# Stick-breaking attention with the keys on the partitions: suffix sums by triangle matmuls

## The chip, the cores and the metric

The kernel runs on one core of a Trainium2 chip. The metric is device time in microseconds of one execution, the median of three runs. A profile shows one execution: its span runs from the first to the last instruction, and its own time is a little longer than the span.

## The reference, cut to what matters

The kernel is one decoder block on a sequence of 1024 tokens with 1024 channels, in float32: a conditioned norm, one wide input projection, a state-space branch and an attention branch beside each other, a gated merge, an output projection, and a feed-forward part. The change concerns the attention branch alone: 8 heads of 64 channels, strictly causal, with stick-breaking weights instead of a softmax:

```python
z = einsum('bhqd,bhkd->bhqk', qb, kh) * scale
mask = key_pos < q_pos
log_not = where(mask, log_sigmoid(-z), 0.0)
suffix = cumsum(log_not, axis=3, reverse=True) - log_not
weights = where(mask, exp(log_sigmoid(z) + suffix), 0.0)
out = einsum('bhqk,bhkd->bhqd', weights, vh)
```

For each query, the log of "stick not broken" is summed over all later keys. With s = softplus(z) = max(z, 0) + ln(1 + exp(-|z|)), log_sigmoid(-z) is -s and log_sigmoid(z) is z - s, so the weight of a key is exp(z minus the sum of s over that key and all later ones).

## The kernel before, in words

The block is built in Python and compiled with a framework that tracks tiles, inserts the waits, and orders each engine's instructions by a plan on simulated times. Program order gives priority; work that comes later in the program fills gaps as soon as its inputs, buffers and manual order allow. A manual order (the helper `after`) holds in the plan only and puts no wait into the program.

Precise matrix products are made from a rounded high part and a remaining low part of each operand (type fp32r, one pass) as three products: high x high, high x low, low x high. Scores and weights times values use plain fp32 matmuls, of which each appears as two instructions.

The attention stage handles the heads in four pairs (`hp`), two heads of a pair side by side (index `x`) in the upper and lower 64 rows or columns. For each pair, `heads` goes over four blocks `I` of 256 queries (the last pair in the order 1, 3, 2, 0), and `scores` (line 679) makes the weights of one block, with **queries on the partitions and keys along the free axis**. A block's scores are cut into units of 384 or 512 columns for both heads, 40 units in all. For each unit:

- line 699 and 703: score matmuls into the tile `z` in PSUM (one buffer of two banks), and a matmul of an identity with a mask on the diagonal;
- line 708: ScalarE copies `z` to `wa`; lines 709 and 710: VectorE makes |z| (`we`) and max(z, 0) (`wr`); lines 711 and 712: ScalarE makes ln(1 + exp(-|z|)) in `we`;
- line 715: VectorE scans both with adds along the keys, from the last key back, which gives the inclusive suffix sum in `wr`; a unit starts from the column where the one before ended (line 719 saves it);
- line 722: GpSimd subtracts it from the scores; line 723: ScalarE takes the exponential.

The product with the values needs the keys on the partitions. So `heads` transposes the weights in 128x128 pieces on TensorE (line 745, into three PSUM buffers `wtp`), copies them out (line 749, on ScalarE, every fourth on VectorE), and multiplies by `V` (line 755) into `av`. Line 758 splits the result into high and low parts.

Between this lies other work for TensorE, which the plan uses to fill gaps: the query and key projections of the next pair (`qk_proj`, pinned after a score matmul of the pair before by `QPIN`), which go through the one PSUM bank `mm`, and the eight gate projections (`gate`, lines 649 to 660, pinned along the stage by `PINS`), which go through the bank `mg_`. Both run on line 622. After the stage, `branch_b` projects the attention's output (line 886). It uses the banks `mm`, `mg_`, the three of `wtp` and the one of `av`.

## Time and profile before

| | us |
|---|---|
| three runs, median (lowest, highest) | 1612.36 (1609.24, 1612.84) |
| the profiled execution, its own time | 1616.59 |
| its span | 1614.7 |
| mean granted TensorE clock of the profiled execution | 0.952 |
| attention stage, from the first score matmul to the last weights times values | 415.2 to 770.5 |
| TensorE busy, of the span | 1462.5 |

In the views that follow, PE is TensorE's matmuls and PEld its weight loads, DVE is VectorE, ACT ScalarE, POOL GpSimd, SP SyncE. The granted clock is a share of TensorE's full speed. A group is all instructions of one line, engine, operation and tile name, and the line of a helper (622, for instance) can serve many callers. In a group's row, the busy time and the mean time of one instruction come first, and after the second bar the time in which the engine stood idle just before them and what ended it. In a list of waits, each row gives who waited for whom, the total, the number of times and the longest. Matmuls are pipelined: the time of one in a row is longer than the distance from one to the next.

### The profile page before, as it was taken

To read this page: it belongs to the slowest core of one execution; us is meant where nothing else is said; L and a number is where in the kernel's file an instruction comes from. 1 tells how busy PE (TensorE), PEld (TensorE's weight loads), DVE (VectorE), ACT (ScalarE), POOL (GpSimd) and SP (SyncE) were. 2 spreads that over 40 slices of the span, in tenths; PEclk is the share of its full clock that TensorE was granted. 3 is DMA by queue.
4 is the path that set the end of the run, shared out by engine and by line. 5 is a ranking of instruction groups with operands and counts; after the bars stand their busy time and mean duration, and the time that the engine had idled before them with its cause. 6 is when DMAs were issued, how large, how long until landed. Compare 5 with 4: busy or idle time off the path is not lost.

```text
span 1614.7 us, 18727 instructions
## 1 busy us (share of the span) xinstructions
PE 1462.5 (91%) x6802; PEld 1149.4 (71%) x6802; DVE 1149.4 (71%) x1402; ACT 616.2 (38%) x859; POOL 790.4 (49%) x591
## 2 busy tenths in 40 slices
PE   4897888899999999889999979999999998999965
PEld 3687776778756666556878758888888886887854
DVE  6988777543576667585742887666566759999978
ACT  4521110352455555465423543332322324343313
POOL 3457784010334243333430454545555468788784
PEclk9998998999999989999999979999999999999988
DMA  8585556634201121201643323333333146455302
GB/s 235 170 197 166 157 161 171 180 120 156 92 7 52 34 78 46 72 24 60 230 176 97 112 67 110 98 100 114 116 119 112 63 158 247 147 159 163 98 27 105
DMA packets 191141, 193.58 MB, mean 120 GB/s; under 512 B 28068, under 2 KB 141832, under 8 KB 191048
## 3 DMA queue, kind: packets, MB, share of 16 engines
q1 hardware_dynamic: 179976, 184.38, 37.1%
q10 hardware_dynamic: 11072, 8.00, 1.7%
q8 instruction: 54, 0.88, 0.2%
q14 instruction: 39, 0.32, 0.1%
HBM read 142.40 MB, written 48.76 MB: 118 GB/s over the span
## 4 chain that ended last, share of the span: by engine, by line
PE 27%; DVE 14%; issue 7%; POOL 5%; DMA 2%; ACT 2%; SPq 0%; DVEq 0%; POOLq 0%; ACTq 0%
PE tq L1041 10%; PE wo L1041 8%; PE wo L922 4%; PE gu L1041 3%; DVE wr L715 1%; POOL wb L1114 1%; DVE x L1129 1%; DVE f L1116 1%; POOL pb L1133 1%; POOL pa L1094 1%; DMA gb<-gD 1%; DVE pb L1129 1%; DVE wl L1112 1%; PE mm L622 1%; DVE we L709 1%
## 5 line engine op out<-in xcount | busy, mean ns | idle before, releaser
L722 POOL TENSOR_TENSOR wa<-wa,wr 128x1024 f32<-128x1024 f32 (+1 forms) x40 | 90.4, 2259 | 183.6 <-DVE wr L715 151.3
L433 POOL TENSOR_TENSOR ws<-wb 128x1024 f32<-128x1024 f32 x29 | 73.2, 2525 | 103.5 <-DVE wl L436 58.6
L715 DVE TENSOR_TENSOR_SCAN wr<-we,wr 128x512 f32<-128x512 f32 (+3 forms) x80 | 79.5, 1042 | 37.6 <-ACT we L712 37.0
L433 POOL TENSOR_TENSOR wgs<-wb 128x1024 f32<-128x1024 f32 x15 | 37.9, 2524 | 101.2 <-DVE x L436 33.4
L709 DVE TENSOR_SCALAR we<-wa 128x1024 int32<-128x1024 int32 (+1 forms) x40 | 53.5, 1338 | 28.4 <-ACT wa L708 28.4
L622 PE MATMUL mm<-pb,wh 128*128 128x512 f32 x192 | 63.2, 407 | 4.1 <-DVE gst L657 4.1
L622 PE MATMUL mm<-pa,wgh 128*128 128x512 f32 x176 | 61.6, 428 | 5.5 <-DVE gst L657 5.5
L1094 POOL TENSOR_TENSOR pa<-pa,row 128x1024 f32<-128x1024 f32 x22 | 64.9, 2975 | 1.5 <-DMA pa<-in_w_ffn_down_dram 1.5
L622 PE MATMUL mm<-pa,wh 128*128 128x512 f32 x192 | 64.1, 413 | 0.1
L1032 POOL TENSOR_TENSOR f<-f,f 128x512 f32<-128x512 f32 x30 | 49.1, 1662 | 26.0 <-DVE f L1022 17.5
L622 PE MATMUL mm<-pb,wgh 128*128 128x512 f32 x176 | 59.0, 413 | 2.6 <-ACT gst L659 2.6
L774 DVE SCALAR_TENSOR_TENSOR acc<-aw,cond,acc 128x512 f32<-128x512 f32 x56 | 52.4, 935 | 12.4 <-DMA aw<-in_w_ada_dram 11.8
L723 ACT ACTIVATE wa<-wa 128x1024 f32<-128x1024 f32 (+1 forms) x40 | 38.8, 971 | 57.4 <-POOL wa L722 57.4
L710 DVE TENSOR_SCALAR wr<-wa 128x1024 f32<-128x1024 f32 (+1 forms) x40 | 60.3, 1507 | 0.0
L755 PE MATMUL av<-wt,V 128*64 128x256 f32 (+1 forms) x320 | 55.5, 384 | 5.1 <-ACT wt L749 1.8
L745 PE MATMUL wtp<-ident,wa 128*128 128x128 f32 x288 | 49.5, 300 | 10.5 <-ACT wa L723 10.5
L711 ACT ACTIVATE we<-we 128x1024 f32<-128x1024 f32 (+1 forms) x40 | 38.9, 972 | 52.1 <-DVE we L709 52.1
L745 PEld LDWEIGHTS wtp<-ident,wa 128*128 128x128 f32 x288 | 34.5, 150 | 32.6 <-ACT wa L723 13.0
L417 POOL TENSOR_TENSOR wl<-ws,wh 128x1024 fp32r<-128x1024 f32 x10 | 25.1, 2516 | 64.4 <-ACT wh L414 64.4
L414 ACT CAST wh<-ws 128x1024 fp32r<-128x1024 f32 x30 | 31.3, 1048 | 65.5 <-PE wo L922 25.7
L699 PE MATMUL z<-k,q 64*128 64x512 f32 (+3 forms) x192 | 46.4, 545 | 4.3 <-ACT wa L708 2.4
L1114 POOL TENSOR_TENSOR wb<-pa 128x512 f32<-128x512 f32 x23 | 40.7, 1777 | 15.6 <-DVE wxl L1112 5.5
(739 smaller groups left out, 4781.4 us busy)
## 6 DMA issues: line engine op xcount, KB each, us to landing
aw<-in_w_ada_dram SPq DMA_DIRECT2D x32, 512.0 KB, 4.6
hD<-f SPq DMA_DIRECT2D x30, 512.0 KB, 3.1
wb<-in_w_ffn_gate_dram SPq DMA_DIRECT2D x44, 256.0 KB, 3.8
wb<-in_w_ffn_up_dram SPq DMA_DIRECT2D x44, 256.0 KB, 4.2
pa<-in_w_ffn_down_dram SPq DMA_DIRECT2D x22, 512.0 KB, 5.8
wb<-hD SPq DMA_DIRECT2D x40, 256.0 KB, 2.8
ws<-in_w_in_dram SPq DMA_DIRECT2D x19, 512.0 KB, 5.9
x<-in_x_dram SPq DMA_DIRECT2D x16, 512.0 KB, 7.1
```

The costliest lines, as they stand in the source:

```text
L433: (add or nc.gpsimd).tensor_tensor(st, a, b, op)
L622: self.nc.tensor.matmul(ps, lhsT=w[a][:, k], rhs=act[h][k][:, b], start=(j == 0), stop=(j == n - 1))
L709: nc.vector.tensor_scalar(s.bitcast(I32), a.bitcast(I32), 0x7FFFFFFF, None, ALU.bitwise_and)
L710: nc.vector.tensor_scalar(r, a, 0.0, None, ALU.max)
L715: nc.vector.tensor_tensor_scan(r[:, x, b:e][:, ::-1], s[:, x, b:e][:, ::-1], r[:, x, b:e][:, ::-1], nxt[x][j], ALU.add, ALU.add)
L722: nc.gpsimd.tensor_tensor(a, a, r, ALU.subtract)
L745: nc.tensor.transpose(ps[:, d, j], w[j][kb // 4][:, x, c:c + P], self.ident)
L755: nc.tensor.matmul(av[h, P * j.start:256], lhsT=V[:, kb + d, h], rhs=ts[x][:, d, j].rearrange("p j q -> p (j q)"), start=(kb + d == 0), st ...
L922: nc.tensor.matmul(ps, lhsT=mg[t // 4][k][:, a, P * (t % 4):P * (t % 4) + P], rhs=ws[k // 2][b][:, k % 2], start=(j == 0), stop=(j == 23))
L1041: self.nc.tensor.matmul(ps, lhsT=w[x][:, q, k], rhs=self.B[i](y, k), start=(j == 0), stop=(j == 11))
L1094: nc.gpsimd.tensor_tensor(w, w, g2, ALU.mult)
L1114: nc.gpsimd.tensor_tensor(st[:, R], u, W[p][b[0]][:, 512 * b[1]:512 * b[1] + 512], SIGN_B[i])
```

## The change

Scores are now made with **keys on the partitions and queries along the free axis**: the operands of the score matmul change places. `heads` goes over two blocks `Q` of 512 queries, and within each over the blocks of 128 keys from the last to the first; the two narrowest blocks at the diagonal share a unit. The softplus s is made as one tile (absolute value on ScalarE straight from PSUM, a copy of z on VectorE, exponential and logarithm on ScalarE, max and add on VectorE), and is rounded into a high and a low part.

The sum over later keys then runs along the partitions and is a matmul. A tile `acc` in PSUM (one bank for each head) holds a running sum. For each key block, a matmul with a triangle of ones (`upto`) adds the block's inclusive suffix sums; VectorE subtracts `acc` from the scores; and a matmul with the complement (`rest`) adds what is missing, so that every row holds the full sum of the block before the next one starts. The exponential of the result has the keys on the partitions already, so it goes straight into the product with `V`.

The scans, the GpSimd subtraction, the transposes and their copies are gone. Score tiles have two buffers in PSUM (four banks), `acc` has two banks, `av` takes the bank `mg_`, and the gates now go through `mm`, the same bank as the query and key projections. `branch_b` gets six banks of its own beside `mm` and `mg_`. The pins are set anew for 40 marks (one for each unit) in place of 64, and the last pair's order of blocks is as in the other pairs.

```diff
-ZPB, WTB, AVB = 1, 3, 1
-WEB, WRB, GB = 2, 2, 2
-WAB2, WTS = 5, 3
+ZPB = 2
+GB = 2
+WAB2, WSB, WHB = 4, 2, 2
-QPIN = -16
-PINS = (0, 8, 16, 24, 32, 40, 48, 56)
-HD = (0, 4)
-HORD = {3: (1, 3, 2, 0)}
+QPIN = -10
+PINS = (0, 5, 10, 15, 20, 25, 30, 35)
...
+    def triangles(self, pool):
+        tri = pool.tile([P, P], F32, name="tri")
+        nc.gpsimd.memset(tri, 1.0)
+        nc.gpsimd.affine_select(out=tri, in_=tri, compare_op=ALU.is_gt, fill=0.0, base=1, pattern=[[-1, P]], channel_multiplier=1)
+        self.upto, self.rest = (pool.tile([P, P], F32R, name=n) for n in ("upto", "rest"))
+        nc.vector.tensor_copy(self.upto, tri)
+        nc.vector.tensor_scalar(self.rest, tri, -1.0, 1.0, ALU.mult, ALU.add)
...
+    def scores(self, q, k, Q, kbs, work):
...
+                ins = nc.tensor.matmul(z[:, x, f:f + w], lhsT=k[h, P * kb:P * kb + P], rhs=q[h, 512 * Q + c:512 * Q + 512],
+                                       start=f == 0, stop=not diag)
...
+        nc.scalar.activation(st, z, AF.Abs)
+        nc.vector.tensor_copy(at, z)
+        nc.scalar.activation(st, st, AF.Exp, scale=-1.0)
+        nc.scalar.activation(st, st, AF.Ln, bias=1.0)
+        nc.vector.scalar_tensor_tensor(st, at, 0.0, st, ALU.max, ALU.add)
+        nc.scalar.copy(ht, st)
+        nc.vector.tensor_tensor(lt, st, ht.bitcast(F32), ALU.subtract)
+        return a, (hi, lo), segs
...
+        for Q in range(2):
+            kbs = [(4 * Q + 3, 4 * Q + 2), (4 * Q + 1,), (4 * Q,)] + [(kb,) for kb in reversed(range(4 * Q))]
+            acc = self.accp.tile([P, 2, 512], F32, name="acc")
+            av = self.avp.tile([P, 512], F32, name="mm")
+            for unit in kbs:
+                a, parts, segs = self.scores(q, k, Q, unit, work)
+                for kb, f, c in segs:
+                    first, last = kb == 4 * Q + 3, kb == 0
                     for x in range(2):
+                        for n in range(2):
+                            nc.tensor.matmul(acc[:, x, c], lhsT=self.upto, rhs=parts[n][:, x, f], start=first and n == 0, stop=last and n == 1,
+                                             skip_group_check=True)
+                        nc.vector.tensor_tensor(a[:, x, f], a[:, x, f], acc[:, x, c], ALU.subtract)
+                        if not last:
+                            for n in range(2):
+                                nc.tensor.matmul(acc[:, x, c], lhsT=self.rest, rhs=parts[n][:, x, f], start=False, stop=False,
+                                                 skip_group_check=True)
+                    self.last_exp = nc.scalar.activation(a[:, :, f], a[:, :, f], AF.Exp)
                     for x in range(2):
                         h = slice(64 * x, 64 * x + 64)
+                        nc.tensor.matmul(av[h, c], lhsT=V[:, kb, h], rhs=a[:, x, f], start=first, stop=last, skip_group_check=True)
+            s = slice(512 * Q, 512 * Q + 512)
             self.split(hi[:, s], lo[:, s], av)
...
-                            self.gate(1, m, gp, self.marks[PINS[m]] if m else None, self.wring[2], mg_)
+                            self.gate(1, m, gp, self.marks[PINS[m]] if m else None, self.wring[2])
...
-                    banks = Turns((mm, "mm"), (mg_, "mm"), *[(self.wtp, "wtp")] * WTB, *[(self.avp, "av")] * AVB)
+                    bb = s3.enter_context(self.pool("bb", 6, PSUM))
+                    banks = Turns((mm, "mm"), (mg_, "mm"), *[(bb, "bb")] * 6)
```

More of the change, by code (lines that the diff above doesn't have):

```diff
@@ L753, in heads @@
                     for x in range(2):
                         h = slice(64 * x, 64 * x + 64)
-                        nc.tensor.matmul(av[h, P * j.start:256], lhsT=V[:, kb + d, h], rhs=ts[x][:, d, j].rearrange("p j q -> p (j q)"),
-                                         start=(kb + d == 0), stop=(last and d == 1))
-            s = slice(256 * I, 256 * I + 256)
+                        nc.tensor.matmul(av[h, c], lhsT=V[:, kb, h], rhs=a[:, x, f], start=first, stop=last, skip_group_check=True)
@@ L1239, in run @@
                     op = s3.enter_context(self.pool("o", 4))
-                    self.zp, self.wtp, self.avp = (s3.enter_context(self.pool(n, b, PSUM)) for n, b in (("zp", ZPB), ("wtp", WTB), ("avp", AVB)))
-                    with self.pool("work", 1) as work, self.pool("wt", WTS) as wt:
+                    with self.pool("tri", 1) as tri, self.pool("work", 1) as work, self.pool("zp", ZPB, PSUM) as self.zp, self.pool("acc", 1, PSUM) as self.accp:
+                        self.avp = mg_
+                        self.triangles(tri)
                         self.marks = []
@@ L1252, in run @@
                             ops.append((t[:, 0], t[:, 1]))
-                            self.heads(hp, q, k, V, work, wt, *ops[hp])
+                            self.heads(hp, q, k, V, work, *ops[hp])
                         spare = []
```

95 lines of the change are left out of this document (25 added, 70 removed).

## The prediction, made blind

> **What bounds the kernel now.** I read the page's busy line first, then the busy time by stretch inside the attention stage, then the list of waits there, then the groups of that stage by line. The attention stage runs from the first score matmul at 415 us to about 766 us, where the projection of line 886 has begun. The change rewrites this stage and touches little else.
>
> ```profile
> PE 1462.5 (91%) x6802; PEld 1149.4 (71%) x6802; DVE 1149.4 (71%) x1402; ACT 616.2 (38%) x859; POOL 790.4 (49%) x591
> ```
>
> TensorE is the fullest engine of the kernel, but that is an average. The stage itself, as busy time by stretch (wall, then busy time and count of PE, PEld, DVE, ACT, POOL, then the granted clock):
>
> ```profile
> 480.00:498.70 18.70, 14.93 (x73) 9.11 (x71) 13.05 (x13) 12.34 (x17) 5.45 (x4) 1.00 0.37 98
> 498.70:505.60 6.90, 5.93 (x19) 5.06 (x20) 6.90 (x6) 3.94 (x6) 6.24 (x3) 0.51 0.10 38
> 505.60:560.00 54.40, 53.48 (x278) 34.73 (x276) 35.92 (x43) 31.99 (x49) 17.32 (x8) 1.00 0.09 25
> 560.00:570.40 10.40, 7.72 (x40) 4.91 (x38) 5.61 (x7) 5.80 (x8) 3.72 (x3) 1.00 0.01 2
> 570.40:580.60 10.20, 9.92 (x30) 6.34 (x31) 10.09 (x9) 6.02 (x7) 6.94 (x3) 0.50 0.65 180
> 580.60:640.00 59.40, 59.40 (x296) 39.95 (x296) 38.72 (x42) 31.98 (x49) 22.91 (x11) 1.00 0.17 54
> 415.00:766.00 351.00, 323.48 (x1551) 212.41 (x1552) 238.89 (x245) 198.07 (x284) 132.85 (x61) 0.94 0.15 45
> ```
>
> The last row is the whole stage: 351.0 us, PE busy 323.5, so 27.5 us idle. The mean clock of 0.94 means another 0.06 x 351 = 21 us in which PE worked at half rate and should not have had to. I call the sum, 48.5 us, the slack of the stage. The other rows show how the two hang together: PE idles 3.8 us in 480 to 498.7, and the next 6.9 us are granted half the clock; it idles 2.7 us in 560 to 570.4, and the next 10.2 us are at 0.50. The long stretches in between are full (59.40 of 59.40) at clock 1.00. Half clock here follows idling. In both half-clock stretches DVE is the full engine (6.90 of 6.90, 10.09 of 10.20). So the stage is bound by PE's work for most of its length, and in short pieces by the scan path behind it:
>
> ```profile
> POOL wa L722 <- DVE wr L715: 151.3, 33, 8.2
> ACT wa L723 <- POOL wa L722: 57.4, 24, 5.4
> PEld wtp L745 <- ACT wa L723: 13.0, 7, 5.7
> PE wtp L745 <- ACT wa L723: 10.5, 5, 4.9
> ```
>
> That is the chain: the scan (715) releases the subtraction on POOL (722), that the exponential (723), that the transposes (745). PE's largest wait, 10.5 us in five pieces, stands at its end.
>
> **The change part by part: PE.** The score matmuls keep their number and their widths with queries and keys exchanged: per pair of heads 24 of them, 12 of 512 columns and 4 each of 384, 256 and 128, as before; the 64 mask matmuls stay too. They cost nothing new. The rest needs these groups and prices (groups of the stage; then pieces of the chain with start, length and count; then one line of the timeline):
>
> ```profile
> L755 PE MATMUL av<-wt,V 128*64 128x256 f32 (+1 forms) x312 | 54.6, 385 | 5.1 <-ACT wt L749 1.8 <-DVE wt L749 1.6 <-DVE o L809 1.5
> L745 PE MATMUL wtp<-ident,wa 128*128 128x128 f32 x288 | 49.5, 300 | 10.5 <-ACT wa L723 10.5
> ```
>
> ```profile
> 683.97 1.01 PE av L755 x8
> ...
> 685.57 0.58 PE av L755 x2
> 686.15 1.02 PE wtp L745 x8
> ...
> 965.76 8.16 PE wo L1041 x36
> ```
>
> Removed: 288 transposes. Packed, one takes 1.02/8 = 0.1275 us, so 288 x 0.1275 = 36.7 us of work; what else stands in the group's 49.5 us is waiting and half clock, which I count as slack.
>
> Added: the suffix sums. Each key block of each head takes two matmuls with the triangle (high and low part), and all but the last block of a sweep two more with its complement. Per pair of heads that is 48 + 40 = 88, in all 352: 160 of 512 columns and 64 each of 384, 256 and 128. They are full-array fp32r matmuls like those of line 1041, where one of 512 columns takes 8.16/36 = 0.227 us. By columns the 384 wide one is 0.170; for 256 and 128 I take the 0.1275 of a packed 128 wide transpose as the floor. 160 x 0.227 + 64 x 0.170 + 128 x 0.1275 = 36.3 + 10.9 + 16.3 = 63.5 us.
>
> By the Trainium skill, "TensorE: Matmul & The Clock Gate", section "Back-to-back issue gap", a sustained stream needs about 131 ns per matmul at 512 columns and 81 ns at 128. An estimate from that page alone would make the added work about 37 us and the removed 23, a net of 14 where my rows give 27. The trace disagrees with its 131 ns: 36 matmuls in a row need 227 ns each, and I stay with the rows.
>
> Weights times values: the same columns in 96 matmuls of up to 512 instead of 160 of up to 256. An fp32 matmul is two instructions, and the two heads sit in different column halves of the array. Eight instructions for two key blocks of both heads take 1.01 us, so one block of both is 0.505; two instructions for one head alone take 0.58. The halves run side by side when both heads are ready together and cost double when not. Before, the heads' transposed copies come from separate evacuations, and the group is busy 54.6 us, where 64 x 0.505 + 16 x 0.25 = 36.3 would do if all were paired. After, both heads' weights come out of one exponential, so they always go as a pair. The gain lies between 0 and 18; I take 10, because some of the excess is half clock and must not be counted twice.
>
> PE's work: +63.5 - 36.7 - 10 = **+17 us** (+9 to +27 by the bounds of the last term).
>
> **The change part by part: DVE, ACT, POOL.** Their groups in the stage:
>
> ```profile
> L722 POOL TENSOR_TENSOR wa<-wa,wr 128x1024 f32<-128x1024 f32 (+1 forms) x40 | 90.4, 2259 | 183.6 <-DVE wr L715 151.3 <-DVE cy L719 13.4 <-ACT wa L708 9.4
> L715 DVE TENSOR_TENSOR_SCAN wr<-we,wr 128x512 f32<-128x512 f32 (+3 forms) x80 | 79.5, 1042 | 37.6 <-ACT we L712 37.0
> L710 DVE TENSOR_SCALAR wr<-wa 128x1024 f32<-128x1024 f32 (+1 forms) x40 | 60.3, 1507 | 0.0
> L709 DVE TENSOR_SCALAR we<-wa 128x1024 int32<-128x1024 int32 (+1 forms) x40 | 53.5, 1338 | 28.4 <-ACT wa L708 28.4
> L715 DVE TENSOR_TENSOR_SCAN wr<-we,cy,wr 128x512 f32<-128x512 f32 x16 | 19.6, 1269 | 7.8 <-ACT we L712 7.7
> L749 DVE COPY wt<-wtp 128x512 f32<-128x512 f32 (+2 forms) x29 | 13.0, 474 | 26.6 <-PE wtp L745 14.5 <-PE av L755 12.1
> L711 ACT ACTIVATE we<-we 128x1024 f32<-128x1024 f32 (+1 forms) x40 | 38.9, 972 | 52.1 <-DVE we L709 52.1
> L712 ACT ACTIVATE we<-we 128x1024 f32<-128x1024 f32 (+1 forms) x40 | 38.9, 972 | 0.6
> L723 ACT ACTIVATE wa<-wa 128x1024 f32<-128x1024 f32 (+1 forms) x40 | 38.8, 971 | 57.4 <-POOL wa L722 57.4
> L708 ACT COPY wa<-z 128x1024 f32<-128x1024 f32 (+1 forms) x40 | 37.1, 927 | 16.1 <-PE wtp L745 7.9 <-PE z L703 5.5 <-PE z L699 2.6
> L749 ACT COPY wt<-wtp 128x512 f32<-128x512 f32 (+2 forms) x83 | 32.6, 442 | 20.4 <-PE wtp L745 14.9 <-PE av L755 5.4
> L414 ACT CAST wh<-ws 128x1024 fp32r<-128x1024 f32 x8 | 8.3, 1046 | 0.0
> L657 DVE COPY gst<-mm 128x512 f32<-128x512 f32 x8 | 5.4, 680 | 8.6 <-PE mm L622 8.6
> ```
>
> ```profile
> 953.86 1.13 DVE wl L436
> ```
>
> ```profile
> 414.50 0.69 DVE L855 TENSOR_TENSOR gst<-ga,sg 128x512 f32<-128x512 f32 x1 [3.17 <-DMA nD<-gst]
> ```
>
> The number of units (score tiles) stays 40, of the same sizes: 24 with 1024 elements, 16 with 768. DVE loses 79.5 + 60.3 + 53.5 + 19.6 + 13.0 = 225.9 us. It gains per full unit a copy out of PSUM (twice the 0.68 of line 657 at most, say 1.3), a max-and-add and a subtraction of 1024 elements (1.13 each, the row of line 436) and two subtractions out of PSUM (0.69 each, line 855): 4.9 us; a smaller unit three quarters of that. 24 x 4.9 + 16 x 3.7 = 177 us, so DVE sheds about 49 and comes to 190 of 351. Its share cannot bind on average.
>
> ACT sheds the 32.6 of line 749 and gains the rounding copy, 24 x 1.05 + 16 x 0.79 = 37.7: +5, to about 203 us. The absolute value takes the place of the copy of line 708 at its price. POOL sheds 90.4 us, and its 2.3 us step falls out of each unit's chain. All three lie beside PE, which has over 320 us of work; they count only through the slack. The two triangles are four small instructions made once, and needed only after the first unit's six operations on ACT and DVE, about 1 us each by the rows above.
>
> New waits: PE's complement matmuls wait until DVE has read the running sum, and stand in PE's queue ahead of whatever follows, fillers (gate and query/key projections) included; DVE's subtraction can itself stand behind one 1.13 us operation. Both heads have a bank of their own, so the other head and the fillers can go in between. The projections of gates and queries/keys now share one bank: 28 evacuations, each beside attention work, so I cost them at nothing; without that cover it would be 28 x 0.7 = 20 us.
>
> **The sum.** The question is what is left of the 48.5 us of slack. The stalls sat where DVE was full and at the end of the scan-POOL-exponential chain; DVE gets 49 us lighter, POOL leaves the chain, two score tiles instead of one may be open. The new sum brings waits of its own. I take half, 24 us left, as the middle between none (a full PE, as in the stretches at 59.40 of 59.40) and all. Stage: 351 + 17 - 24.5 = 343.5, **-7.5 us**. Against the profiled execution's 1616.6 that is 1609; the median of the three runs lies 4.2 below the profiled one, so I predict **1605 us**.
>
> **The rivals.** (a) *The new sum stalls PE as the scan did*: slower. Its place is the 80 pairs of complement matmuls, which PE meets in order behind DVE's 0.69 us read and what DVE does before. If they wait 0.3 us each on average, 80 x 0.3 = 24 us come back, the slack stays at 48.5, and +17 of work is paid in full: 1612.4 + 17 = 1629; with unpaired heads, +27, 1639. It decides from a mean wait of about 0.1 us (8 us) upwards. For it: 27.5 us of idle now arise from just such handovers. Against: PE has projections of line 622 to put between (the same view, that line alone): 672 x 0.227 = 152 us of them.
>
> ```profile
> 415.00:766.00 351.00, 180.15 (x672) 127.96 (x672) 0.94 0.15 45
> ```
>
> (b) *All slack goes*: PE full, 5 us left: 351 + 17 - 43.5 = -26, 1586. For it: the full stretches; against: start and tail of the stage, where fillers are short. (c) *The clock alone*: if the transposes, not the idling, kept the clock down, taking them out would bring back 21 us with the idle time unchanged: +17 - 21 = -4, 1608. The Trainium skill, "TensorE: Matmul & The Clock Gate", Part 4, says that transposes don't count as busy for the clock. The trace speaks against it: 50 transposes (line 745 alone, below) lie in a stretch granted 1.00 throughout, and both shown drops follow idling.
>
> ```profile
> 580.60:640.00 59.40, 7.88 (x50) 5.51 (x50) 1.00 0.17 54
> ```
>
>  (d) *Nothing to measure*: work gained and slack lost cancel, 1612 within 3. That the edit doesn't do what it says can be left out: the instructions it names are gone or there.
>
> **How the numbers follow.** Forecast 0.34 (1592 to 1609), (b) 0.13, (c) 0.04, (d) 0.15, (a) 0.34. 0.2% is 3.2 us, about what a measurement here can tell. Faster: 0.34 + 0.13 + 0.04 less a little of the near end, 0.49; same 0.15; slower 0.36. Both signs hold much of the chance: the likeliest case's own range is 1592 to 1609. The range of all: down into (b), 1588; up into (a) past its 1629, 1634. The lower part of (b), and (a) with unpaired heads, stay out, about 2 in 10.
>
> **What would show it.** In the profile after: line 745's group gone, the triangle matmuls near 60 us at full clock; weights times values down from 54.6 towards 40; DVE in the stage near 190, POOL near 45; PE's idle time in the stage near 14 and its clock near 0.97. It is wrong if PE waits on DVE's subtraction for more than 20 us in all, if the stage stays at a clock of 0.94, if DVE's operations take well over 1.13 us, or if the tail after the last scores leaves PE idle for over 15 us.

## The result, and the profile after

| | before | changed |
|---|---|---|
| median of 11 runs each, side by side, us | 1609.71 | 1618.39 |
| lowest, highest | 1604.66, 1613.67 | 1613.42, 1624.63 |
| ratio (95% interval) | 1 | 1.0053 (1.0035 to 1.0071) |
| profiled execution: own time, span | 1616.59, 1614.7 | 1618.39, 1616.7 |

The change makes the kernel slower by 8.7 us, 0.5%, and the interval of the ratio lies clear of 1. The forecast was 1605 us, faster.

The two profiled executions differ by 1.8 us only, and that misleads. Up to the first score matmul the matmuls of both kernels stand in the same order, yet that part, which waits on transfers, lasted 415.3 us in the profile of before and 404.6 in that of the changed kernel; over all profiles of this study it lies between 402.4 and 415.5. So I compare from the first score matmul on. From there to the first matmul of the output projection (tile `wo`) the kernel before takes 399.2 us and the changed one 414.5, which is 15.3 more. From `wo` to the end of the span they take 800.2 and 797.6. The difference of the two is 12.7 us, a little more than the 8.7 of the medians; a second profile of the changed kernel, below, gave 415.9 from the first score matmul to `wo` and a ratio of 1.0078. Each such time comes from one profiled execution.

The page's busy line after:

```profile
PE 1475.8 (91%) x6738; PEld 1153.8 (71%) x6738; DVE 1106.9 (68%) x1399; ACT 626.6 (39%) x816; POOL 705.3 (44%) x553
```

PE gained 13 us of busy time over the page of before, DVE lost 43 and POOL 85: what was to become lighter did. Busy time by stretch of the stage, first score to last weights times values, in the changed kernel (columns as in the prediction):

```profile
404.60:440.00 35.40, 34.92 (x147) 24.07 (x148) 15.53 (x16) 17.95 (x22) 6.92 (x3) 0.81 0.18 52
440.00:480.00 40.00, 32.95 (x143) 18.54 (x144) 28.12 (x35) 29.50 (x34) 5.03 (x2) 0.96 0.00 1
480.00:520.00 40.00, 39.14 (x183) 25.85 (x181) 20.73 (x27) 20.64 (x25) 0.00 (x0) 1.00 0.15 40
520.00:560.00 40.00, 32.46 (x132) 16.72 (x131) 29.19 (x35) 32.51 (x37) 5.47 (x2) 0.91 0.08 27
560.00:580.00 20.00, 20.00 (x91) 13.60 (x90) 10.65 (x13) 11.57 (x13) 0.00 (x0) 1.00 0.08 27
580.00:740.00 160.00, 158.09 (x716) 108.67 (x715) 79.16 (x99) 78.30 (x93) 24.41 (x14) 1.00 0.19 61
740.00:769.50 29.50, 25.66 (x103) 14.48 (x101) 17.57 (x21) 18.49 (x19) 1.28 (x1) 1.00 0.07 27
404.60:769.50 364.90, 343.22 (x1506) 221.93 (x1506) 200.96 (x241) 208.96 (x242) 43.11 (x22) 0.97 0.14 43
```

The same from first score to last weights times values in the kernel before, a little longer than the stretch in the prediction:

```profile
415.20:770.50 355.30, 327.98 (x1575) 215.69 (x1575) 238.69 (x244) 199.33 (x286) 132.65 (x61) 0.94 0.16 48
```

By the prediction's way of counting, the slack before is 355.3 - 328.0 = 27.3 us of idle and 0.06 x 355.3 = 21.3 of half clock, 48.6 together; after, 364.9 - 343.2 = 21.7 and 0.03 x 364.9 = 10.9, 32.6 together. It fell by 16 us. What is left of the wall is PE's work: 306.7 before, 332.3 after, 25.6 more. The stage is 9.6 us longer for it. (The clock is printed with two digits, so a half-clock term, and with it the work, is good to about 2 us.) Some 7 us of the 10.9 lie at the head of the stage, where the first 14 us were granted 0.52 while PE was full (404.60 to 418.60, 13.99 of 14.00 busy), behind 1.8 us of idling ahead of the first score matmul; that part stands ahead of any wait for the new sum.

Two stretches hold most of the idle time, 440 to 480 and 520 to 560. PE works 32.95 and 32.46 of 40 us there, and no other engine is full either: DVE stands at 28 and 29, ACT at 30 and 33. Where nobody is full, the engines may be waiting for one another. The list of waits in the stage names whom:

```profile
DVE wa L738 <- PE acc L736: 87.0, 49, 6.0
ACT wa L743 <- DVE wa L738: 67.6, 27, 8.7
PEld acc L741 <- DVE wa L738: 27.9, 31, 2.2
PE acc L741 <- DVE wa L738: 12.2, 16, 1.8
```

Line 736 is the triangle, 738 the subtraction, 741 the complement, 743 the exponential. DVE waits for the triangles, PE for the subtraction, and both for each other within one key block, first for one head and then for the other. PE's 12.2 us are the largest part of its 21.7 us of idle time. (PE's and PEld's waits overlap and are not to be added.) Groups of the stage:

```profile
L738 DVE TENSOR_TENSOR wa<-wa,acc 128x512 f32<-128x512 f32 (+3 forms) x96 | 52.9, 552 | 87.5 <-PE acc L736 87.0
L717 DVE SCALAR_TENSOR_TENSOR ws<-wa,ws 128x1024 f32<-128x1024 f32 (+1 forms) x40 | 48.2, 1208 | 16.9 <-ACT ws L716 16.7
L719 DVE TENSOR_TENSOR wl<-ws,wh 128x1024 fp32r<-128x1024 f32 (+1 forms) x40 | 46.0, 1150 | 13.0 <-ACT wh L718 12.3
L746 PE MATMUL mm<-wa,V 128*64 128x512 f32 (+3 forms) x192 | 42.7, 524 | 1.3 <-ACT wa L743 1.2
L736 PE MATMUL acc<-wh,upto 128*128 128x512 f32 (+3 forms) x96 | 34.6, 360 | 1.6 <-DVE wa L738 1.6
L741 PE MATMUL acc<-wh,rest 128*128 128x512 f32 (+3 forms) x80 | 31.3, 392 | 12.5 <-DVE wa L738 12.2
```

Weights times values went from 54.6 us to 42.7. I call the way from the triangle on PE to the subtraction on DVE and back to the complement on PE a trip. It is in the timeline, PE and DVE at one narrow block at the diagonal:

```profile
525.99 1.22 DVE L714 COPY wa<-z 128x1024 f32<-128x1024 f32 x1
526.22 0.30 PE L736 MATMUL acc<-wh,upto 128*128 128x128 f32 x1 [1.41 <-DVE wa L738]
526.36 0.28 PE L736 MATMUL acc<-wl,upto 128*128 128x128 f32 x1
...
527.13 0.95 DVE L719 TENSOR_TENSOR wl<-ws,wh 128x768 fp32r<-128x768 f32 x1
...
527.99 0.28 DVE L738 TENSOR_TENSOR wa<-wa,acc 128x128 f32<-128x128 f32 x1
...
528.52 0.47 PE L741 MATMUL acc<-wh,rest 128*128 128x128 f32 x1
...
529.00 0.41 PE L736 MATMUL acc<-wh,upto 128*128 128x128 f32 x1
...
529.28 1.23 DVE L717 SCALAR_TENSOR_TENSOR ws<-wa,ws 128x1024 f32<-128x1024 f32 x1 [1.01 <-ACT ws L716]
...
530.43 0.28 DVE L738 TENSOR_TENSOR wa<-wa,acc 128x128 f32<-128x128 f32 x1
...
531.47 0.33 PE L741 MATMUL acc<-wh,rest 128*128 128x128 f32 x1
```

One head's triangle starts at 526.22, its complement at 528.52; the other head's start at 529.00 and 531.47. That is 4.8 us of trips for two reads of 0.28. In the first, the subtraction stands behind a copy and the making of a low part; in the second behind the max-and-add, before which DVE stood still for 1.01 us until ACT's logarithm came, and which started at 529.28, just after the second of the two triangle matmuls (at 529.22). PE is not idle for all of this: scores (at 527.27) and weights times values (at 529.56) stand in between. It idles for 1.41 us before the first triangle, which waits for the subtraction ahead of it, and for 0.64 before the scores.

### The profile page after: what moved, and what is told of

Same layout as the page of the kernel before. It is cut to its first block, busy times and chain, and to the rows that moved or that the text cites. A ratio compares the mean times of both kernels' runs of the same rounds, so it can differ in the third digit from the quotient of the medians.

```text
span 1616.7 us, 18487 instructions
## 1 busy us (share of the span) xinstructions
PE 1475.8 (91%) x6738; PEld 1153.8 (71%) x6738; DVE 1106.9 (68%) x1399; ACT 626.6 (39%) x816; POOL 705.3 (44%) x553
## 4 chain that ended last, share of the span: by engine, by line
PE 49%; DVE 21%; issue 9%; POOL 8%; DMA 8%; ACT 5%; SPq 1%; ACTq 0%; DVEq 0%; POOLq 0%
PE mm L619 11%; PE tq L1031 10%; PE wo L1031 8%; PE wo L912 5%; PE ga L619 3%; PE gu L1031 3%; PE z L699 2%; DVE acc L559 2%; PE mm L746 2%; DMA aw<-in_w_ada_dram 2%; PE acc L736 2%; PE acc L741 1%; DVE acc L764 1%; DVE x L1119 1%; POOL pb L1123 1%
## 5 line engine op out<-in xcount | busy, mean ns | idle before, releaser
L738 DVE TENSOR_TENSOR wa<-wa,acc 128x512 f32<-128x512 f32 (+3 forms) x96 | 52.9, 552 | 87.5 <-PE acc L736 87.0
L413 POOL TENSOR_SCALAR wgh<-wgs 128x1024 fp32r<-128x1024 f32 x8 | 8.7, 1092 | 206.8 <-PE mm L619 146.1
L743 ACT ACTIVATE wa<-wa 128x1024 f32<-128x1024 f32 (+3 forms) x48 | 40.4, 842 | 67.8 <-DVE wa L738 67.6
L714 DVE COPY wa<-z 128x1024 f32<-128x1024 f32 (+1 forms) x40 | 44.6, 1116 | 29.1 <-ACT ws L713 18.0
L1022 POOL TENSOR_TENSOR f<-f,f 128x512 f32<-128x512 f32 x30 | 50.1, 1694 | 26.8 <-DVE f L1012 18.3
L717 DVE SCALAR_TENSOR_TENSOR ws<-wa,ws 128x1024 f32<-128x1024 f32 (+1 forms) x40 | 48.2, 1208 | 16.9 <-ACT ws L716 16.7
L411 ACT CAST wh<-ws 128x1024 fp32r<-128x1024 f32 x30 | 31.4, 1046 | 63.8 <-PE wo L912 27.6
L764 DVE SCALAR_TENSOR_TENSOR acc<-aw,cond,acc 128x512 f32<-128x512 f32 x56 | 46.9, 837 | 12.2 <-DMA aw<-in_w_ada_dram 11.7
L719 DVE TENSOR_TENSOR wl<-ws,wh 128x1024 fp32r<-128x1024 f32 (+1 forms) x40 | 46.0, 1150 | 13.0 <-ACT wh L718 12.3
L699 PE MATMUL z<-q,k 64*128 64x512 f32 (+3 forms) x192 | 48.3, 574 | 4.8 <-DVE wa L714 2.9
L713 ACT ACTIVATE ws<-z 128x1024 f32<-128x1024 f32 (+1 forms) x40 | 37.4, 936 | 33.6 <-DVE wl L719 32.4
L718 ACT CAST wh<-ws 128x1024 fp32r<-128x1024 f32 (+1 forms) x40 | 38.3, 957 | 28.9 <-PE acc L741 22.5
L1011 ACT ACTIVATE f<-f 128x1024 f32<-128x1024 f32 x22 | 23.4, 1061 | 62.3 <-DVE f L1051 32.5
```

Source lines behind the costliest of these rows:

```text
L699: ins = nc.tensor.matmul(z[:, x, f:f + w], lhsT=k[h, P * kb:P * kb + P], rhs=q[h, 512 * Q + c:512 * Q + 512], start=f == 0, stop=not diag)
L714: nc.vector.tensor_copy(at, z)
L717: nc.vector.scalar_tensor_tensor(st, at, 0.0, st, ALU.max, ALU.add)
L719: nc.vector.tensor_tensor(lt, st, ht.bitcast(F32), ALU.subtract)
L738: nc.vector.tensor_tensor(a[:, x, f], a[:, x, f], acc[:, x, c], ALU.subtract)
L764: nc.vector.scalar_tensor_tensor(acc, w[:, j], cj, acc, ALU.mult, ALU.add)
```

## The experiments

The theory: the trips PE, DVE, PE make the stall, because there are two of them in a row for each key block and the subtraction waits in DVE's queue. Its rivals: the fillers stand in the wrong place since gates and query/key projections share a bank; the end of the stage is bare, because of the new order of the last pair; or PE simply has more to do. Each ratio below is against the kernel before, run beside it; "z to wo" is the time from the first score matmul to the first of the output projection, 399.2 us before and 414.5 after. "PE's own wait for the subtraction" is the wait of the complement matmuls in the list for engine PE: 12.2 us in the first profile of the changed kernel, 10.9 in the second. All edits but one (e3) are made to the changed kernel.

**e1, gates between the pairs.** In the changed kernel every gate matmul comes after the third query/key projection in the program, and one bank keeps that order. The first row is the gates' part of it up to 580 us (windows of the tile with the high part of the gates' weights; its matmuls are two in three of a gate's), the second the rest of the stage:

```profile
404.60:580.00 175.40, 0.00 (x0) 0.00 (x0) 0.00 (x0) 0.00 (x0) 1.56 (x1) 0.93 0.10 29
580.00:769.50 189.50, 81.31 (x256) 46.93 (x256) 0.00 (x0) 0.00 (x0) 24.41 (x14) 1.00 0.17 56
```

In the kernel before, 103 lay before 580:

```profile
415.20:580.00 164.80, 36.54 (x103) 20.66 (x104) 0.00 (x0) 0.00 (x0) 12.57 (x7) 0.94 0.14 40
```

The edit puts two gates behind each pair:

```diff
+GATES = ((0, 1), (2, 3), (4, 5), (6, 7))
...
-                            if hp:
-                                qk.append(self.qk_proj(hp, qp, kp, self.marks[QPIN]))
...
                             self.heads(hp, q, k, V, work, *ops[hp])
+                            if hp < 3:
+                                qk.append(self.qk_proj(hp + 1, qp, kp, self.marks[QPIN]))
+                            for m in GATES[hp]:
+                                self.gate(1, m, gp, self.marks[PINS[m]] if m else None, self.wring[2])
...
-                        for m in range(KT):
-                            self.gate(1, m, gp, self.marks[PINS[m]] if m else None, self.wring[2])
```

> The changed kernel, with the program order of the fillers alone altered: the query and key projections of the next pair and two of the eight gate projections are issued after each pair of heads, so that in the one bank they share the gates no longer stand behind the third query and key projection. Theory C (the fillers stand in the wrong half: the gates all run after 580 us, and PE stalls where it has none): the idle time of PE between 440 and 580 us goes, the stage comes down from 365 to 340 to 350 us, ratio to the kernel before 0.990 to 0.998. Theory A (the running sum's handshake with VectorE stalls PE by itself): the waits of the complement matmuls stay near 40 us in all, ratio 1.003 to 1.008 as in the changed kernel.

Measured: 1.0097 (1.0080 to 1.0114), z to wo 416.7: no gain. The gates did move (first row, that tile alone), and the early stretches filled; the idle time moved to where filler had been taken away (second and third row, all instructions):

```profile
402.40:580.00 177.60, 41.39 (x128) 23.35 (x128) 0.00 (x0) 0.00 (x0) 12.79 (x7) 0.98 0.14 41
...
460.00:480.00 20.00, 19.38 (x93) 14.24 (x92) 9.59 (x11) 9.35 (x11) 3.44 (x2) 1.00 0.22 65
...
740.00:760.00 20.00, 14.22 (x36) 6.16 (x36) 13.68 (x15) 11.49 (x12) 0.00 (x0) 0.74 0.00 1
```

PE's own wait for the subtraction rose to 18.6 us. By itself the place of the fillers is not the cause. It seems that there is not enough of them to cover the trips everywhere; e12 bears on that.

**e2, a bank for the gates.** One score tile instead of two pays for it.

```diff
-ZPB = 2
+ZPB = 1
...
+                    with ..., self.pool("gb", 1, PSUM) as gb:
...
-                            self.gate(1, m, gp, self.marks[PINS[m]] if m else None, self.wring[2])
+                            self.gate(1, m, gp, self.marks[PINS[m]] if m else None, self.wring[2], gb)
```

> The changed kernel, with a PSUM bank of their own for the gate projections, paid for with one score tile instead of two (ZPB 1). Theory C: the gates spread over the whole stage again, the stalls between 440 and 580 us go, less what the single score tile costs: ratio 0.990 to 1.002. Theory A: handshake waits as before and one buffer less: ratio 1.005 to 1.015.

Measured: 1.0159 (1.0138 to 1.0179), z to wo 423.2. Worse than the changed kernel by about 1%. The gates did spread: 128 of the 256 matmuls with the high part lie before 580. Losing a score tile and gaining a bank are not told apart here; together they cost.

**e3, the kernel before with one bank.** The reverse: the kernel before, its gates moved into the bank of the query/key projections.

```diff
-                            self.gate(1, m, gp, self.marks[PINS[m]] if m else None, self.wring[2], mg_)
+                            self.gate(1, m, gp, self.marks[PINS[m]] if m else None, self.wring[2])
```

> The kernel before, with one part of the change alone: the gate projections go through the bank of the query and key projections. Theory C: the gates are held back behind the third query and key projection and pile up at the end of the stage, ratio 1.005 to 1.025 with nothing else changed. Theory A: the bank does not matter, ratio 0.998 to 1.002.

Measured: 1.0181 (1.0161 to 1.0202), z to wo 426.9, 27.7 us more. More than half of the gates' matmuls pile up behind the last scores at 718.8 (the gates' tile alone):

```profile
718.80:815.00 96.20, 48.60 (x146) 28.30 (x146) 1.23 (x1) 1.52 (x2) 13.65 (x8) 0.96 0.37 126
```

So an edit that I had costed at nothing is dear in the kernel before, where the stage needs those fillers. In the changed kernel nothing piles up behind the stage: all 256 of these matmuls lie inside it, as the rows above show.

**e4, the last pair's blocks in reverse.**

```diff
-        for Q in range(2):
+        for Q in ((1, 0) if hp == 3 else (0, 1)):
```

> The changed kernel, with the two blocks of 512 queries of the last pair of heads taken in the other order, the short one last. Theory T (the long block at the end leaves a tail in which PE starves, and holds back the projection behind it): the time from 740 us to the first matmul of the output projection falls by 3 to 6 us, ratio 1.001 to 1.004. If the tail costs nothing: 1.005, as the changed kernel. Theories A and C expect no more than that either.

Measured: 1.0100 (1.0079 to 1.0120), z to wo 414.9: nothing gained. The order at the end of the stage is not the cause.

**e5, the changed kernel again,** unaltered, beside the three experiments that follow.

> The changed kernel once more, beside the next three on one chip. If the first part of the program (identical in order in both kernels, and 11 us apart in the two profiles) only varies from run to run, the ratio to the kernel before lies between 1.004 and 1.011, and the stage takes 362 to 368 us.

Measured: 1.0078 (1.0051 to 1.0105), z to wo 415.9. Its stage has 19.6 us idle and 18.4 of half clock, 38 us of slack where the first profile had 32.6, so two profiles of one kernel differ here by 5 us:

```profile
410.00:778.00 368.00, 348.40 (x1506) 224.81 (x1506) 201.14 (x241) 209.42 (x242) 43.10 (x22) 0.95 0.14 43
```

**e6, a short read.** The subtraction on 64 columns of each piece alone.

```diff
-        nc.vector.tensor_copy(at, z)
+        nc.vector.tensor_scalar(at, z, 0.0, None, ALU.min)
...
-                        nc.vector.tensor_tensor(a[:, x, f], a[:, x, f], acc[:, x, c], ALU.subtract)
+                        fs, cs = slice(f.start, f.start + 64), slice(c.start, c.start + 64)
+                        nc.vector.tensor_tensor(a[:, x, fs], a[:, x, fs], acc[:, x, cs], ALU.subtract)
```

> The changed kernel, in which VectorE's subtraction reads and writes only the first 64 columns of each piece (the other columns go on without the sum, and the copied scores are cut at zero so that all stays finite). The matmuls are all there. Theory A (what holds PE is the step from the triangle to the complement by way of VectorE): each step is about 0.4 us shorter and VectorE 35 us lighter, the complement's waits fall below 10 us in all, the time falls by 12 to 35 us against the changed kernel. Theory W (PE pays its 20 us of added work, and the waits are what they were before): 0 to 5 us less.

Measured: 1.0050 (1.0031 to 1.0068) against 1.0078 (1.0051 to 1.0105), z to wo 408.6, 7 us less than the changed kernel beside it; the totals' intervals overlap. That is less than I expected of the theory. The subtraction got 0.34 us shorter (217 ns against 552 in the first profile), but PE's own wait for it only went from 10.9 to 9.3 us, and DVE's wait for the triangles is as long as ever, 91.9 us where it was 87.0 in the first profile:

```profile
L739 DVE TENSOR_TENSOR wa<-wa,acc 128x64 f32<-128x64 f32 x96 | 20.8, 217 | 92.4 <-PE acc L736 91.9
```

The trips of the timeline took 2.3 and 2.5 us with a read of 0.28; most of a trip is the standing in queues. With the totals' intervals overlapping, this run by itself decides nothing.

**e7, a double read.**

```diff
-                        nc.vector.tensor_tensor(a[:, x, f], a[:, x, f], acc[:, x, c], ALU.subtract)
+                        for _ in range(2):
+                            nc.vector.scalar_tensor_tensor(a[:, x, f], acc[:, x, c], -0.5, a[:, x, f], ALU.mult, ALU.add)
```

> The changed kernel, in which VectorE subtracts half the sum twice, so that each step from the triangle to the complement is 0.55 us longer and VectorE has 53 us more to do; TensorE's work is the same. Theory A: 15 to 45 us more than the changed kernel. Theory W: 0 to 5 us more, since VectorE stays at 260 of 365 us.

Measured: 1.0489 (1.0469 to 1.0508), z to wo 477.4, 61.5 us more than the changed kernel beside it and more than expected. The group doubled to 190 operations and 105.0 us, 52 more than before; the stage went to a clock of 0.87:

```profile
L739 DVE SCALAR_TENSOR_TENSOR wa<-acc,wa 128x512 f32<-128x512 f32 (+3 forms) x190 | 105.0, 553 | 111.8 <-PE acc L736 109.5
```
```profile
410.70:839.00 428.30, 376.95 (x1505) 233.14 (x1505) 251.68 (x337) 212.15 (x242) 42.60 (x22) 0.87 0.12 37
```

DVE is busy 251.7 of 428.3 us, so its share does not bind. The 52 us put on the trips come back as 61 us of time, half clock included, and PE's own wait for the subtraction went from 10.9 to 29.1 us. The theory asks for a loss here, and the rivals named above do not. But the edit also gives VectorE 52 us more to do, so it does not tell a longer trip from a busier VectorE; e10 does.

**e8, high part only.** The triangles' and complements' matmuls with the low part are left out: half of the added work of PE, and a shorter trip by one matmul on each side.

```diff
-                        for n in range(2):
-                            nc.tensor.matmul(acc[:, x, c], lhsT=self.upto, rhs=parts[n][:, x, f], start=first and n == 0, stop=last and n == 1,
+                        for n in range(1):
+                            nc.tensor.matmul(acc[:, x, c], lhsT=self.upto, rhs=parts[n][:, x, f], start=first, stop=last,
...
-                            for n in range(2):
+                            for n in range(1):
```

> The changed kernel with the sums made from the high part alone: half of the 352 triangle and complement matmuls are left out, about 31 us of TensorE's work, while each step by way of VectorE stays. Theory W: the time falls by 25 to 31 us against the changed kernel. Theory A: by 8 to 20 us, since a part of the matmuls left out lay in gaps that stay as waits.

Measured: 0.9998 (0.9986 to 1.0010), z to wo 402.2, 13.7 us less. Half of the added work is 31 us, so more than half of the relief did not arrive:

```profile
406.60:759.30 352.70, 324.26 (x1330) 198.53 (x1330) 203.51 (x241) 209.51 (x242) 44.53 (x22) 0.92 0.14 44
```

Idle is 28.4 and half clock 28.2 here: the slack rose to 56.6 us from 38. PE's work is not the only bound; what stands behind it comes forward as soon as it shrinks. The time lies in the range expected of the theory (8 to 20 us less), not in that of PE's work alone (25 to 31).

**e10, both heads' trips together.** If the number of trips in a row is the cost, one trip for both heads halves it: all four triangles, both subtractions, then all four complements.

```diff
                     for x in range(2):
                         for n in range(2):
                             nc.tensor.matmul(acc[:, x, c], lhsT=self.upto, ...)
+                    for x in range(2):
                         nc.vector.tensor_tensor(a[:, x, f], a[:, x, f], acc[:, x, c], ALU.subtract)
-                        if not last:
-                            for n in range(2):
-                                nc.tensor.matmul(acc[:, x, c], lhsT=self.rest, ...)
+                    for x in range(0 if last else 2):
+                        for n in range(2):
+                            nc.tensor.matmul(acc[:, x, c], lhsT=self.rest, ...)
```

> The changed kernel with the loop over the two heads taken apart: first the triangle matmuls of both heads, then both subtractions, then the complements of both. Same instructions, same results; each key block has one trip from TensorE to VectorE and back for both heads in place of two, one after the other. Theory A (the trips of the running sum set the pace where no filler is there): the time falls by 8 to 20 us against the changed kernel's 1.0078, ratio 0.995 to 1.003, and PE's waits for the subtraction halve. Theory W (PE's added work): no change, 1.005 to 1.010.

Measured: 0.9997 (0.9981 to 1.0013), z to wo 401.7, 13 to 14 us less than the changed kernel, with the same instructions in another order. The stage itself shrank from 365 to 309 us (first row, all instructions). Much of this is work put off: half of the gates are left to do after the last scores at 688.6 (second row, the gates' tile alone), and those that come after the stage lengthen the way to `wo`, 93 us from the last weights times values where the changed kernel has 50. The rest is slack: 13.1 us idle and 3.1 of half clock, 16.2 together, where the two profiles of the changed kernel have 32.6 and 38, and that with fewer fillers in the stage. PE's own wait for the subtraction is 7.8 us, less than before but not half of it. VectorE's work is unchanged, so it is the trips and not VectorE's load that this run relieves:

```profile
412.50:721.60 309.10, 296.00 (x1355) 190.03 (x1355) 198.98 (x236) 204.36 (x239) 33.92 (x17) 0.99 0.13 41
...
688.60:790.00 101.40, 42.45 (x130) 25.60 (x130) 3.96 (x2) 2.08 (x2) 13.19 (x8) 0.93 0.39 128
```

**e11, one subtraction for both heads,** the rest as in e10.

```diff
-                    for x in range(2):
-                        nc.vector.tensor_tensor(a[:, x, f], a[:, x, f], acc[:, x, c], ALU.subtract)
+                    nc.vector.tensor_tensor(a[:, :, f], a[:, :, f], acc[:, :, c], ALU.subtract)
```

> As the run before, with one subtraction of VectorE for both heads in place of two: one fixed cost less for each of the 48 key blocks, but the first head's sum now waits for the second's. Theory A: within 4 us of the run before. If VectorE's time counts by itself: 4 to 6 us less than the run before.

Measured: 0.9985 (0.9969 to 1.0001), z to wo 396.2. Not to be told from the one above by the totals. In z to wo it is 5.5 us less, one profile against one, so the run does not decide between its two expectations.

**e12, trips together and gates between.** The edits of e10 and e1 in one kernel: now that the trips are half as many, the fillers should be enough.

> Both edits at once: the heads taken together, and two gate projections issued after each pair of heads (as in the run with gates between). Theory A: the trips are shorter and fillers stand in all four pairs, 3 to 8 us less than the heads taken together alone, ratio 0.990 to 1.000. If the place of the fillers does not matter, as the first run of it says: within 3 us of the heads taken together alone.

Measured: 1588.93 us, 0.9877 (0.9854 to 0.9899), z to wo 379.6. It beats both kernels, by 20 us and more, and e10 by 20 us, more than either expectation allowed. The stage as a whole, then the gates' tile alone before 580 us and behind the last scores at 713.6:

```profile
415.50:746.20 330.70, 327.60 (x1501) 217.73 (x1501) 205.68 (x241) 206.90 (x242) 44.53 (x22) 0.99 0.16 47
...
415.50:580.00 164.50, 33.78 (x104) 19.38 (x105) 0.00 (x0) 0.00 (x0) 12.17 (x7) 0.98 0.16 45
...
713.60:790.00 76.40, 10.02 (x32) 5.93 (x32) 2.44 (x2) 2.09 (x2) 0.00 (x0) 0.96 0.47 158
```

PE is busy 327.6 of 330.7 us at 0.99: 6.4 us of slack. Its own wait for the subtraction is down to this:

```profile
PE acc L743 <- DVE wa L740: 2.0, 2, 1.1
```

A trip in its timeline, with PE's projections (line 620) now in between:

```profile
440.40 0.44 PE L737 MATMUL acc<-wh,upto 128*128 128x384 f32 x1
...
440.68 0.34 PE L737 MATMUL acc<-wl,upto 128*128 128x384 f32 x1
...
440.85 0.34 PE L737 MATMUL acc<-wh,upto 128*128 128x384 f32 x1
...
441.03 0.33 PE L737 MATMUL acc<-wl,upto 128*128 128x384 f32 x1
...
441.20 0.39 PE L620 MATMUL mm<-pb,wl 128*128 128x512 f32 x1
...
442.03 1.01 DVE L740 TENSOR_TENSOR wa<-wa,acc 128x384 f32<-128x384 f32 x2
...
447.66 0.33 PE L743 MATMUL acc<-wh,rest 128*128 128x384 f32 x1
```

The four triangles run one behind the other, the two reads too, and PE goes on with filler from 441.20 until the first complement at 447.66. From the first triangle to there it is 7.3 us, three times the 2.3 and 2.5 us of the changed kernel's trips shown above, and PE idles for only 0.69 us of it (before a projection at 442.97). So this trip's length costs next to nothing, because PE has something to put into it.

**e13, all three.** e12 with the one subtraction of e11.

> The heads taken together, two gate projections issued after each pair of heads, and one subtraction of VectorE for both heads. With the trips together and the fillers spread, PE idles for only a few microseconds in the stage, so what VectorE saves should no longer show: within 3 us of the run with both edits (ratio 0.986 to 0.990). If the trip still sets the pace somewhere, 3 to 8 us less than that run (0.983 to 0.986).

Measured: 1593.54 us, 0.9905 (0.9888 to 0.9922), z to wo 384.6. That is just above the 0.990 expected, with an interval that meets e12's. The single subtraction adds nothing; e12 stays the best.

Not tested is the number of buffers for the two parts of the softplus: in the changed kernel ScalarE waits 22.5 us for a complement matmul (line 718 on 741) before it can write the next high part.

## Why the prediction was wrong

*The sum inside the stage.* I had PE's work at +17 and the slack at -24.5. The first profile has +25.6 and -16, so each of the two terms missed by some 8.5 us, to within the 2 us of the clock's digits. Behind the stage another 5.8 us came, which I had not forecast.

*The work of PE: right in the prices, too small in the sum.* Where two of a kind follow each other at full clock, the median distance from start to start is 0.111, 0.120, 0.176 and 0.233 us for triangles and complements of 128, 256, 384 and 512 columns, which makes 63.4 us for the 352 (63.5 predicted), and 0.109 us for the transposes, 31.4 us for 288 (36.7 predicted). For the rest of this paragraph each matmul is counted from its start to the next start or to its own end, whichever comes first, times the granted clock. Weights times values so counted went from 49.0 to 38.5 us (10 less predicted). By these numbers I should have found +21.5. But the triangles and complements do not stand packed: the 352 take 76 us in the changed kernel, and 69 in e12, which has them in rows of four instead of two. So what failed in this term is the price of a row of 36, set on matmuls that come in twos. The windows say the same: 25.6 us more work in the first profile, 23 in the second (368.0 - 38.0 = 330.0 against 306.7), 17.6 in e12 (330.7 - 6.4 = 324.3). A likely way, which no run took apart, is that short bursts pay for their start: in e12's timeline the second triangle comes 0.28 us after the first, the third and fourth 0.17 and 0.18 after the one ahead.

*DVE, ACT, POOL.* The directions were right. DVE is at 201 us in the stage, not 190. A full max-and-add and a full low part take 1.22 and 1.26 us where I took 1.13 from another line, and most of the excess lies in the smaller units, whose operations took 70 us where my three quarters of a full unit made 59. ACT is at 209 (203), POOL at 43 (45). None of it binds by its share, as said; but DVE's operations count by the place in its queue.

*The failed step: "I take half, 24 us left"* of the slack. It was a middle between two ends without a mechanism. The slack fell by 16 us in the first profile, by 11 in the second, against the 24.5 in the sum. The scan's stall went as forecast; another took its place, and the prediction had named it as rival (a), with place and mechanism: PE's wait for the subtraction. Its deciding point was a mean wait of 0.1 us over the 80 pairs; 12.2 / 80 = 0.15 on PE's own list. So (a) came true in part: some of the slack went all the same. The result, 1618, lies between the forecast and its 1629. The argument against it, 152 us of projections to put between, failed: the trips come two in a row for each of 40 key blocks (80 pairs, two heads), and e1 shows that spreading the fillers only moves the bare stretches. What I should have costed is one trip in full, from the triangle's start to the complement's (triangle, what stands ahead in DVE's queue, read): by the prediction's own rows that is 2 x 0.227 + 1.13 + 0.69 = 2.3 us, twice for a key block of 512 columns, where I had let "DVE's subtraction can itself stand behind one 1.13 us operation" go by without a sum. The runs bear the trips out as the cause of the stall: with the trips of both heads together, and the same instructions, the slack of the stage is 16.2 us (e10), and with fillers between them besides it is 6.4 (e12).

*A term put at nothing: "28 evacuations, each beside attention work, so I cost them at nothing".* I looked at the evacuations and not at the order that one bank enforces. In the kernel before, that order alone costs 1.8% (e3). For this result it is not shown to count: in the changed kernel another order within the bank gained nothing (e1), and a bank for the gates, paid for with a score tile, lost (e2). It counts once the trips are taken together: e12 against e10, 0.9877 against 0.9997.

*Behind the stage.* From the last weights times values to the first output projection matmul it took 44.3 us before and 50.1 after, and between 48.4 and 51.6 in the profiles of e1, e2, e4 to e8, e12 and e13. I had not forecast it at all. PE's waits there, after:

```profile
PE bb L779 <- ACT wgh L432: 3.2, 1, 3.2
```
```profile
819.10 0.76 PE L912 MATMUL wo<-wh,pa 128*128 128x512 f32 x1 [3.58 <-DVE gb L878]
```

Together 6.8 us. Before, the first was 0.9 and there was no other. I can place this loss, but no experiment took it apart; its cause stays open.

*The rivals (b) and (c).* (b), all slack gone, is not this kernel, but it is what e12 does with two more edits: 6.4 us left where (b) said 5, PE's work at +17.6 where the prediction had +17, and 1588.9 where (b) said 1586. Part of that is luck, since the triangles and complements are dearer in e12 than forecast (69 us for 63.5). (c), the clock held down by the transposes: the clock did rise, 0.94 to 0.97, but 0.95 in the second profile, and e7, which has no transposes either, falls to 0.87 when PE idles more; 0.74 stands in a bare stretch of e1. The half clock came where PE had idled, though not in proportion: 13.7 us of it behind 1.8 us of idling at the head of the changed kernel's stage, 3.4 us behind 2.0 us in the kernel before. The Trainium skill, "TensorE: Matmul & The Clock Gate", section "A second HAM failure mode: psum-queue depth-cycling", tells of short idling between groups of matmuls that sets the clock swinging between half and full. e7's trace agrees: in its stage the granted clock was 0.50 in nine stretches, 109 us together, and 1.00 between them.

*What would have shown it.* The marks I set were too loose one by one: PE's own wait for the subtraction was 12.2, not over 20 (PEld's was 27.9), the clock 0.97, DVE 201, PE's idle time after the last scores well under 15. Line 745's group was gone and weights times values fell to 42.7, as forecast. Only the idle time, 21.7 us where I wanted 14, told.

## What to carry to other kernels

When a sum that ran within one engine becomes an accumulation which another engine reads between its steps, cost the trip, not the operations: count how many follow one another, add what stands ahead in the reading engine's queue, and compare the total with the filler that lies at that place, not with the filler of the whole stage. Send independent trips off together before you try to hide them: in this kernel filler placed between them paid only after that (alone it gave nothing, behind the other edit 1.2%). And a shared PSUM bank costs what it forbids to run earlier, even where its evacuations are covered.

## What the runs showed of the hardware beside this

The length of the reads weighs unequally in the two directions: 32 us less of it (96 x 0.335, e6) gained 7 us up to `wo`, 52 us more of it (e7) lost 61, with the stage's clock going from 0.95 to 0.87 on top of the waiting.

DVE works in order here. In the changed kernel's timeline it stood idle for 0.27 us before line 799, which waited for ACT, although the triangle for the next subtraction had started at 531.92 and ended, as far as the profile models it, at 532.20; the subtraction ran only behind line 799:

```profile
533.15 0.69 DVE L799 TENSOR_TENSOR o<-mm,o 128x512 fp32r<-128x512 f32 x1 [0.27 <-ACT o L798]
533.76 0.41 DVE L738 TENSOR_TENSOR wa<-wa,acc 128x256 f32<-128x256 f32 x1
```

In the second profile (e5) the same line held a subtraction back through 0.92 us of idling: its triangle had ended at 539.66, line 799 started at 540.76, the subtraction at 541.37. The Trainium skill, "Perfetto Trace Analysis", section "Tensor Engine Instruction (MATMUL, LD_WEIGHTS)", says that VectorE, ScalarE and GpSimd are strict FIFOs. For VectorE these timelines agree.
